# A streaming encoder layer on one core: which queue loads the first constants, how the first unit's chain is laid out, how the residual arrives, and who loads head 0

## The chip, the cores and the metric

The kernel runs as one program on one core of a Trainium2 chip. A core has five engines with a queue of instructions each, which is worked through in order: PE (TensorE, the matrix engine), DVE (VectorE), ACT (ScalarE), POOL (GpSimd) and SP (SyncE, which here only issues transfers). Any of SP, ACT and POOL can issue a transfer (DMA); the transfers of all queues are carried by the same 16 DMA engines. An instruction that waits holds up everything behind it on its own engine, and nothing else.

The metric is the device time of one execution in microseconds (us), lower is better. The kernel before has a median of 1366.96 us over three runs (1365.69 to 1368.74).

## The reference

One layer of a hybrid encoder over a prompt of 1024 frames and a sample of 32 frames, 1056 columns of width 1024 in all. Cut to its core:

```python
mod = jax.nn.silu(c) @ w_ada + b_ada
sh1, sc1, g1, sh2, sc2, g2 = jnp.split(mod[:, None, :], 6, axis=-1)
h = x * (1 + sc1) + sh1
mq, mk, mv, mo, mi, mf, fq, fk, fv, ff, gu, gv = jnp.split(h @ w_in, split_at, axis=-1)
hm, (C1, n1, m1) = _mlstm(heads(mq), heads(mk) * HEAD_DIM ** -0.5, heads(mv), li, lf, st0, blk)
hm = _head_norm(hm) * mlstm_norm_g * jax.nn.sigmoid(heads(mo))
hf = _fox_prompt(heads(fq), fk_h, fv_h, logf)      # softmax attention with a forget decay, 8 heads
hg = _spatial_gate(gu, vn, gmlp_ws, gmlp_bs)
mix = jnp.concatenate([hm, hf, hg], axis=-1) @ w_o
x = _layer_norm(ALPHA * x + (1 + g1) * mix, ln1_g, ln1_b)
h = x * (1 + sc2) + sh2
y = (jax.nn.silu(h @ w_gate) * (h @ w_up)) @ w_down
x = _layer_norm(ALPHA * x + (1 + g2) * y, ln2_g, ln2_b)
```

Everything is in float32. A product is made of three matmuls: each operand is split into a high part in the matrix engine's reduced format and the remainder (low), and high x high, high x low and low x high are added up.

## The kernel before

**Layout.** Activations lie transposed: 128 features on the partitions, frames on the free axis. A 1024 x 128 slice of a weight is loaded as one tile of 128 x 1024 (512 KB, `raw`), ACT copies it into the high part (`whi`, line 104) and DVE subtracts to get the low part (`wlo`, line 105). `gemm` (lines 116, 117, 118) then issues three matmuls for each of the eight blocks of the contraction.

**What sets the order.** The program is written once, from top to bottom, for tiles of named pools; a scheduler that goes by its own modelled times then lays each engine's instructions out in one fixed order and sets the semaphores. `issue_after(x)` keeps instructions behind x in that order. A pool's memory may lie where an earlier pool's lay that has been closed; its first writers then wait for the last users of the old tiles.

**The start.** `constants` loads two small tables on SP's queue, `colp` (biases and scales) and `cT` (the condition c), whose silu is needed by every ada unit. `fm_first` makes the first unit of the input projection, for eight blocks k of the contraction: `ada(k)` multiplies c with two halves of `w_ada` (512 KB each, 4 matmuls each, line 178), turns the result with two transposes (line 184), and adds the bias (lines 186, 192); `h1(k)` loads block k of x (540 KB) and makes h = x * (1 + scale) + shift on DVE (lines 216, 217) and its high and low parts on ACT and DVE (lines 221 to 224); then come 18 matmuls for block k. The unit's weights (two loads of 512 KB) are asked for behind block 0's h.

**Up to the first layer norm.** Further units of the projection follow, whose results go to tables in HBM (`dqh`, `dql`, `dmo`, `dmv` and others), then the first mixers (mLSTM, FoX, gMLP) for the first 512 columns. Their outputs come back from HBM with `wo_mix` (tiles `tm_al`, `tm_ah`); `wo_res` fetches the residual x into the 128 x 8 x 512 tile z (`wo_z`) with four loads of 512 KB; `wo_range` multiplies with `w_o` for 8 blocks m, first for columns 0 to 255, then 256 to 511, and `sublayer_end` adds the result to z on DVE (line 1066). `ln1` normalises on DVE and ACT (lines 1083 to 1092), while PE works on the last units of the projection; those are the fm units whose results are copied to the output o_kT by way of the tile `fm_qkr` in pool `sm` (on POOL's or ACT's queue). `ln1_res` then scales z once more on POOL (line 1101, 16 instructions), for the residual of the block after it.

**The second fox.** Pool `mx1` opens on the right side, where `p1` and `sm` lay. `mixers` runs the mixers of the other columns as many small pieces woven into the matmuls of SwiGLU (`up`). `fox(0)` loads head 0's queries, keys and decays with eight transfers and its values with a ninth (lines 747 to 755, SP's queue): qp and k1 first, which the first two score matmuls (line 779) need, then q2 and k2 for the next two (line 780). `mlstm` loads its pieces (`mv`, `mo`, `mb`), again on SP, and prepares the output gate from `mo` on ACT (lines 607 to 609). `ada` goes on in this region: one unit's result is copied by ACT (line 181) and turned on PE (line 184).

Of the kernel before, what the change touches and what calls it, by code (L numbers as in the profile page):

```python
# [63 lines left out]
def f(ap):  # L64
    return ap.bitcast(F32)


class Kernel:
# [14 lines left out]

    def load(self, out, in_):
        self.lastload = self.nc.sync.dma_start(out, in_)
        return self.lastload
# [34 lines left out]
    def constants(self):  # L121
# [48 lines left out]
    def ada(self, u, pool, tag, bufs, ppool, ptag):  # L170
        self.phase = "ada"
        nc = self.nc
        ps = self.t(ppool, [P, 512], F32, ptag)
        for half in range(2):
            raw = self.t(pool, [P, 1024 if tag == "late" else 1056], F32, tag, bufs)[:, :1024]
            self.load(raw, self.d["w_ada"][u, :, half * 1024:(half + 1) * 1024])
            for k in range(4):
                nc.tensor.matmul(ps[32 * k:32 * k + 32, :256], self.c32[:, 4 * half + k, :],
                                 raw[:, k * 256:(k + 1) * 256], start=half == 0, stop=half == 1)
        a = self.t(self.pada, [P, 256], F32, "adas", 2)  # L180
        nc.scalar.copy(a, ps[:, :256])
        pt = ps[:, 256:512]
        for half in range(2):
            nc.tensor.transpose(pt[:, half * P:(half + 1) * P], a[:, half * P:(half + 1) * P], self.ident)
# [23 lines left out]


    def h1(self, k):  # L210
        nc = self.nc
        x = self.t(self.p0, [P, T], F32, "x", XB)
        self.lastx = self.load(x, self.d["xT"][k])
        sh, sc = self.modcol("sh1", k), self.modcol("sc1", k)
# [28 lines left out]
    def fm_first(self, src):  # L243
# [4 lines left out]
                 ((self.pg, "g"), (self.pg, "g"), (self.pg, "g"), (self.pss, "s"), (self.pss, "s"), (self.po, "o"))]  # L248
        w = None
        self.ada(0, self.p0, "araw", AB, self.pt, "t")  # L250
        for k in range(KT):
# [128 lines left out]

    def decay(self, out, h, rows, tiles):
        j0, j1 = tiles
        self.load(f(out).rearrange("p (j q) -> p j q", q=P),
                  self.dfs.rearrange("(j h) r q -> h r j q", h=8)[h, rows, j0:j1])

# [351 lines left out]
    def fox(self, h, chunks):  # L737
# [6 lines left out]
        else:  # L744
            k1, k2, qp, q2, v = self.head_tiles(h, nq, nk)
            qs = slice(q0, q1)
            self.load(f(qp[0:64]), self.dqh[h, 0:64, qs])
            self.load(f(qp[64:128]), self.dql[h, 0:64, qs])
            self.load(f(k1[0:64]), self.dqh[h, 64:128, :nk])
            self.load(f(k1[64:128]), self.dqh[h, 64:128, :nk])  # L750
            self.load(f(q2[0:64]), self.dqh[h, 0:64, qs])
            self.decay(q2[64:68], h, slice(2, 6), (chunks[0][0], nb))
            self.load(f(k2[0:64]), self.dql[h, 64:128, :nk])
            self.decay(k2[64:68], h, slice(0, 4), (0, nb))
            self.load(f(v), self.dv[:, :nb, h * P:(h + 1) * P])
# [287 lines left out]
    def wo_range(self, st, a, b, order, kept, pool):  # L1043
# [293 lines left out]
    def run(self):  # L1337
# [120 lines left out]
        self.wo_mix(0, self.KORDER[0][6:])  # L1458
        self.wo_res(0, self.pz)
        self.pn = self.pool("pn")  # L1460
# [224 lines left out]
```

## Time and profile before

| | |
|---|---|
| median of three runs | 1366.96 us |
| the profiled execution | 1366.61 us, of which 1364.7 us are the span of the trace |
| PE busy | 1330.3 us (97%) |
| DVE, ACT, POOL busy | 995.4 (73%), 656.7 (48%), 226.6 us (17%) |
| granted clock of PE | 0.995 of full speed over the span |

Times in the trace are counted from the start of the span; the 1.9 us around it do not show. "Idle before" in a row of the timeline is the time in which the engine had nothing to do before this instruction, with the instruction or transfer that ended it. PE is idle for 34.4 us in all: 9.28 us in the first 20 us, 2.9 us in 300 to 380, 1.7 us in 380 to 400, 4.9 us in 445 to 462, and 12.15 us behind 1200 us; nowhere else is it more than 1 us in 40.

### The profile page before, as it was taken

What the parts mean: (1) busy time and instruction counts of PE and PEld (TensorE: products, weight loads), DVE (VectorE), ACT (ScalarE), POOL (GpSimd) and SP (SyncE); (2) the same over time, 40 slices, a digit from 0 to 9 for tenths busy, and PEclk for the clock granted to TensorE, in tenths of its full rate; (3) what the DMA queues carried; (4) which work ended last, traced back from release to release, by engine and by line L of the source; (5) the groups of instructions that cost most, each with busy time, mean ns of one, the idle gap of its engine ahead of it and who ended that gap; (6) DMA issues with size and microseconds to landing.
All of it is one profiled execution on the core that took longest, in us unless ns stands there. A gap on an engine that the chain in (4) does not pass through costs nothing.

```text
span 1364.7 us, 25185 instructions
## 1 busy us (share of the span) xinstructions
PE 1330.3 (97%) x9434; PEld 1215.8 (89%) x9434; DVE 995.4 (73%) x2129; ACT 656.7 (48%) x1306; POOL 226.6 (17%) x263
## 2 busy tenths in 40 slices
PE   7999999999999899999999999999999999999996
PEld 4898889998989777888887888999999999999995
DVE  5545553679769667786776765678988988879777
ACT  3314454545536554545545354336664554645355
POOL 0202000053134200000000000373710000000341
PEclk9999999999999899999999999999999999999998
DMA  9765565547454765454344334574596758454321
GB/s 359 273 231 152 161 206 154 163 138 212 134 201 135 207 189 171 119 154 134 109 122 120 104 110 130 156 181 124 164 254 170 205 149 223 146 170 127 99 79 66
DMA packets 119289, 221.70 MB, mean 162 GB/s; under 512 B 18676, under 2 KB 62352, under 8 KB 119168
## 3 DMA queue, kind: packets, MB, share of 16 engines
q1 hardware_dynamic: 111936, 207.55, 48.9%
q0 software_dynamic: 6032, 11.94, 5.1%
q8 instruction: 74, 1.21, 0.4%
q10 hardware_dynamic: 1200, 0.62, 0.2%
q14 instruction: 47, 0.39, 0.1%
HBM read 188.13 MB, written 51.85 MB: 176 GB/s over the span
## 4 chain that ended last, share of the span: by engine, by line
PE 84%; DVE 7%; DMA 5%; ACT 2%; issue 1%; SPq 1%; POOL 1%; DVEq 0%; ACTq 0%
PE up_g L117 5%; PE up_g L118 5%; PE up_g L116 5%; PE dn_g L116 4%; PE dn_g L118 4%; PE dn_g L117 4%; PE tm_g L281 3%; PE tm_g L282 3%; PE tm_g L283 3%; PE sup_u L118 3%; PE sup_u L116 3%; PE sup_u L117 3%; PE fox_t L815 2%; PE sup_g L117 2%; PE sup_g L118 2%; PE sup_g L116 2%
## 5 line engine op out<-in xcount | busy, mean ns | idle before, releaser
L117 PE MATMUL up_g<-tm_al,up_whi 128*128 128x512 f32 (+1 forms) x384 | 141.0, 367 | 0.5 <-DVE tm_al L1092 0.5
L116 PE MATMUL up_g<-tm_ah,up_whi 128*128 128x512 f32 (+1 forms) x384 | 141.2, 369 | 0.2
L118 PE MATMUL up_g<-tm_ah,up_wlo 128*128 128x512 f32 (+1 forms) x384 | 140.5, 366 | 0.0
L1211 ACT CAST sup_whi<-sup_raw 128x1024 fp32r<-128x1024 f32 x54 | 56.0, 1048 | 90.3 <-PE dn_u L117 46.7
L116 PEld LDWEIGHTS up_g<-tm_ah,up_whi 128*128 128x128 f32 x384 | 72.7, 190 | 12.5 <-ACT tm_ah L1091 0.6
L117 PEld LDWEIGHTS up_g<-tm_al,up_whi 128*128 128x128 f32 x384 | 73.1, 190 | 11.1 <-DVE tm_al L1092 0.7
L118 PEld LDWEIGHTS up_g<-tm_ah,up_wlo 128*128 128x128 f32 x384 | 73.2, 191 | 10.7
L788 ACT ACTIVATE fox_p<-fox_s,fox_fmx 128x384 f32<-128x384 f32 (+2 forms) x96 | 55.1, 578 | 44.8 <-DVE fox_fmx L786 37.4
L104 ACT CAST up_whi<-up_raw 128x1024 fp32r<-128x1024 f32 x50 | 52.4, 1048 | 49.7 <-PE up_g L117 19.0
L1212 DVE TENSOR_TENSOR sup_wlo<-sup_raw,sup_whi 128x1024 fp32r<-128x1024 f32 x54 | 68.2, 1267 | 10.5 <-ACT sup_whi L1211 10.5
L1066 DVE SCALAR_TENSOR_TENSOR wo_z<-dn_g,start_mod,wo_z 128x512 f32<-128x512 f32 (+4 forms) x120 | 60.3, 521 | 20.1 <-PE dn_g L118 19.7
L105 DVE TENSOR_TENSOR up_wlo<-up_raw,up_whi 128x1024 fp32r<-128x1024 f32 x50 | 65.7, 1314 | 11.6 <-ACT up_whi L104 11.0
L116 PE MATMUL dn_g<-up_acth,dn_whi 128*128 128x512 f32 (+2 forms) x200 | 74.1, 371 | 0.0
L118 PE MATMUL dn_g<-up_acth,dn_wlo 128*128 128x512 f32 (+2 forms) x200 | 73.4, 367 | 0.0
L117 PE MATMUL dn_g<-up_actl,dn_whi 128*128 128x512 f32 (+2 forms) x200 | 72.9, 365 | 0.0
L820 ACT CAST fox_pth<-fox_t 128x512 fp32r<-128x512 f32 (+1 forms) x80 | 41.0, 545 | 59.5 <-PE fox_t L815 59.3
L104 ACT CAST dn_whi<-dn_raw 128x1024 fp32r<-128x1024 f32 (+1 forms) x44 | 42.7, 971 | 52.2 <-PE up_g L117 10.7
L783 DVE TENSOR_REDUCE fox_fmx<-fox_s 128x1 f32<-128x384 f32 (+2 forms) x96 | 52.7, 553 | 13.0 <-PE fox_s L780 11.8
L821 DVE TENSOR_TENSOR fox_ptl<-fox_t,fox_pth 128x512 fp32r<-128x512 f32 (+1 forms) x80 | 49.5, 631 | 14.5 <-ACT fox_pth L820 14.4
L105 DVE TENSOR_TENSOR dn_wlo<-dn_raw,dn_whi 128x1024 fp32r<-128x1024 f32 (+1 forms) x44 | 49.5, 1125 | 13.7 <-ACT dn_whi L104 13.2
L281 PE MATMUL tm_g<-tm_whi,start_h1h 128*128 128x256 f32 (+1 forms) x192 | 55.3, 288 | 1.7 <-ACT tm_vhl L711 1.7
L282 PE MATMUL tm_g<-tm_wlo,start_h1h 128*128 128x256 f32 (+1 forms) x192 | 55.1, 287 | 0.0
(667 smaller groups left out, 4806.8 us busy)
## 6 DMA issues: line engine op xcount, KB each, us to landing
up_raw<-w_gu SPq DMA_DIRECT2D x50, 512.0 KB
dn_raw<-w_dn SPq DMA_DIRECT2D x28, 512.0 KB
ada_late<-w_ada SPq DMA_DIRECT2D x24, 512.0 KB
sup_raw<-w_gu SPq DMA_DIRECT2D x20, 512.0 KB
start_dp<-w_gu SPq DMA_DIRECT2D x19, 512.0 KB
start_dp<-w_gu POOLq DMA_DIRECT2D x19, 512.0 KB, 7.5
wo_raw<-w_o SPq DMA_DIRECT2D x18, 512.0 KB
sup_raw<-start_dp SPq DMA_DIRECT2D x18, 512.0 KB
```

The lines of the kernel that those rows point to most:

```text
L104: nc.scalar.copy(hi[:, :w], raw[:, :w])
L105: (eng or nc.vector).tensor_tensor(lo[:, :w], raw[:, :w], f(hi[:, :w]), ALU.subtract)
L116: nc.tensor.matmul(ps, hi, xh(k), start=start and k == 0, stop=False)
L117: nc.tensor.matmul(ps, hi, xl(k), start=False, stop=False)
L118: nc.tensor.matmul(ps, lo, xh(k), start=False, stop=stop and k == n - 1)
L281: nc.tensor.matmul(ps[:, :ncol], xh, hi, start=k == 0, stop=False)
L282: nc.tensor.matmul(ps[:, :ncol], xh, lo, start=False, stop=False)
L783: nc.vector.tensor_reduce(mxs[:, x:x + 1], s[:, :w], AX.X, ALU.max, negate=True)
L788: nc.scalar.activation(pr[:, lo:hi], banks[x][:, :hi - lo], AF.Exp, bias=mxs[:, 0:1], accum_out=sums[:, x:x + 1])
L1066: self.lastz = self.nc.vector.scalar_tensor_tensor(z[:, m, x:y], ps[:, x - a:y - a], g[i], z[:, m, x:y], ALU.mult, ALU.add)
L1211: nc.scalar.copy(h, x)
L1212: tt(l, x, f(h), ALU.subtract)
```

## The change

Four places are changed.

1. `constants`: cT and then colp are loaded by ACT's queue instead of SP's.
2. `fm_first`: ada(0) is followed at once by the load of x's block 0 and of the first half of the unit's weights (512 KB, four blocks of the contraction), which is split in four pieces of 256 columns, each with its own copy on ACT and subtraction on DVE. ada(1) stands behind ada(0)'s transposes on PE. The second half of the weights is fetched at k = 3, behind block 3 of x.
3. `wo_res` takes a range of columns and two blocks at a time, 256 KB a load. For columns 0 to 255 these loads stand between the loads of `w_o`; those of the second range behind the weights of m = 5 and m = 7.
4. Head 0's eight loads go by POOL's queue (only those of h = 0; the values' load stays on SP). `ln1_res(0)` is written behind the mixers and after these loads. The pools `sm` and `p1` swap places on the right side, so that the first tiles of `mx1`, head 0's, no longer lie over `sm`.

```diff
+    def load(self, out, in_, eng=None):
+        if eng:
+            self.lastside = eng.dma_start(out, in_)
+            return self.lastside
...
-        self.load(self.colp, d["colp"])
-        self.load(self.ct, d["cT"])
+        nc.scalar.dma_start(self.ct, d["cT"])
+        nc.scalar.dma_start(self.colp, d["colp"])
...
+            self.turned = nc.tensor.transpose(pt[:, half * P:(half + 1) * P], a[:, half * P:(half + 1) * P],
+                                              self.ident)
...
-        w = None
         self.ada(0, self.p0, "araw", AB, self.pt, "t")
+        self.x = self.first_x(0)
+        raw, hi, lo = (self.t(self.wp, [P, 1056], y, x, b) for x, y, b in
+                       (("raw", F32, RAW), ("whi", F32R, WB), ("wlo", F32R, WB)))
+        self.load(raw[:, :1024], src[:, :1024])
+        w = []
+
+        def split(k):
+            c = slice(256 * k, 256 * k + 256)
+            self.nc.scalar.copy(hi[:, c], raw[:, c])
+            self.nc.vector.tensor_tensor(lo[:, c], raw[:, c], f(hi[:, c]), ALU.subtract)
+            w.append((hi[:, c], lo[:, c]))
+
+        split(0)
+        with self.tc.issue_after(self.turned.ins):
+            self.ada(1, self.p0, "araw", AB, self.pt, "t")
         for k in range(KT):
-            if k < KT - 1:
+            if 1 <= k < KT - 1:
                 self.ada(k + 1, self.p0, "araw", AB, self.pt, "t")
             self.h1(k)
-            if w is None:
-                w = self.weights(src, KT, 256)
+            if k == 0:
+                for i in range(1, 4):
+                    split(i)
+            if k == 3:
+                with self.tc.issue_after(self.lastx.ins):
+                    w += self.weights(src[:, 1024:], 4, 256)
...
+            eng = self.nc.gpsimd if h == 0 else None
-            self.load(f(qp[0:64]), self.dqh[h, 0:64, qs])
+            self.load(f(qp[0:64]), self.dqh[h, 0:64, qs], eng)
...
-    def wo_res(self, c, pool):
-        z = self.z[c] = self.t(pool, [P, KT, GN[c]], F32, f"z{c}", 1)
-        for k in range(0, KT, 2):
-            self.load(z[:, k:k + 2], self.d["xT"][k:k + 2, :, GO[c]:GO[c] + GN[c]].rearrange("k p n -> p k n"))
+    def wo_res(self, a, b, k):
+        self.load(self.z[0][:, k:k + 2, a:b], self.d["xT"][k:k + 2, :, a:b].rearrange("k p n -> p k n"))
...
+            if a == 0 and m % 2 == 0:
+                self.wo_res(a, b, m)
             w = kept.get(m) or self.weights(self.d["w_o"][m], KT, P, None, pool if m < 3 else None)
+            if a == 0 and m in (5, 7):
+                with self.tc.issue_after(self.lastload.ins):
+                    for k in ((0, 4), (6, 2))[m // 7]:
+                        self.wo_res(*MM[0][1], k)
...
+        self.sm = self.pool("sm", 2, ctx=s1, side="right")
         self.p1 = self.pool("p1", ctx=s1, side="right")
-        self.sm = self.pool("sm", 2, ctx=s1, side="right")
...
-        self.ln1_res(0)
...
         self.mixers()
+        with tc.issue_after(self.lastside.ins):
+            self.ln1_res(0)
```

The scheduler makes other orders of it. Three places follow; the numbers in the names tell tiles apart and mean nothing else.

**The start, on DVE.** From the mods of unit 0 to the parts of block 0's h. Before:

```order
L186 TENSOR_REDUCE ada_adam_208<-ada_t_191 128x4
L192 TENSOR_SCALAR start_mod_156<-ada_adam_208,start_colp_108 128x2 x2
L216 TENSOR_SCALAR ada_h_235<-ada_x_233,start_mod_156 128x1024
L217 TENSOR_SCALAR ada_h_235<-ada_x_233,start_mod_156 128x32
L186 TENSOR_REDUCE ada_adam_229<-ada_t_212 128x4
L192 TENSOR_SCALAR start_mod_156<-ada_adam_229,start_colp_108 128x2 x2
L222 TENSOR_TENSOR start_al_170<-ada_h_235,start_ah_169 128x512
```

Now:

```order
L269 TENSOR_TENSOR fm_wlo_216<-fm_raw_214,fm_whi_215 128x256
L190 TENSOR_REDUCE ada_adam_208<-ada_t_191 128x4
L269 TENSOR_TENSOR fm_wlo_216<-fm_raw_214,fm_whi_215 128x256
L196 TENSOR_SCALAR start_mod_156<-ada_adam_208,start_colp_108 128x2 x2
L269 TENSOR_TENSOR fm_wlo_216<-fm_raw_214,fm_whi_215 128x256 x2
L225 TENSOR_SCALAR ada_h_241<-ada_x_212,start_mod_156 128x1024
L226 TENSOR_SCALAR ada_h_241<-ada_x_212,start_mod_156 128x32
L231 TENSOR_TENSOR start_al_170<-ada_h_241,start_ah_169 128x512
```

The four subtractions of the weights' first half now stand ahead of h and between the steps of unit 0's mods; unit 1's mods went behind.

**The w_o stage, on SP.** From the last mixer tile on (`dqh`, `dql` are stores of the projection). Before:

```order
L85 DMA tm_al_4640<-start_dmix_32_88 128x512
L85 DMA wo_z_895_4890<-xT 128x2x512 x4
L85 DMA wo_raw_5023<-w_o 128x1024
L85 DMA wo_raw_5060<-w_o 128x1024
L89 DMA start_dqh_57<-fm_qkh_4840 128x272
L85 DMA wo_raw_5097<-w_o 128x1024
```

Now:

```order
L88 DMA tm_al_4646<-start_dmix_32_88 128x512
L88 DMA wo_z_895_4896<-xT 128x2x256 x2
L88 DMA wo_raw_5027<-w_o 128x1024
L88 DMA wo_z_895_4896<-xT 128x2x256
L88 DMA wo_raw_5065<-w_o 128x1024
L88 DMA wo_z_895_4896<-xT 128x2x256
L92 DMA start_dqh_57<-fm_qkh_4846 128x272
L88 DMA wo_raw_5102<-w_o 128x1024
```

Two loads of 256 KB instead of four of 512 KB stand ahead of the first `wo_raw`.

**Head 0 of the second fox, on PE and ACT.** On PE from the last matmuls ahead of the first score (`fox_s`). Before:

```order
L116 MATMUL up_g_7925<-tm_ah_4639,up_whi_7838 128x256
L779 MATMUL fox_s_5854<-fox_k_1018_5837,fox_qp_5839 128x384
L779 MATMUL fox_s_5858<-fox_k_1018_5837,fox_qp_5839 128x256
L117 MATMUL up_g_7900<-tm_al_4640,up_whi_7832 128x256
L118 MATMUL up_g_7900<-tm_ah_4639,up_wlo_7833 128x256
```

Now:

```order
L121 MATMUL up_g_7935<-tm_ah_4645,up_wlo_7849 128x256
L181 MATMUL ada_g_7967<-ada_raw_7974,start_c_63_182 32x256 x4
L808 MATMUL fox_s_5848<-fox_k_1018_5831,fox_qp_5833 128x384
L808 MATMUL fox_s_5852<-fox_k_1018_5831,fox_qp_5833 128x256
L187 MATMUL ada_g_7967<-start_ident_121,ada_adas_7980 128x128 x2
L119 MATMUL up_g_8003<-tm_ah_4645,up_whi_7993 128x512
```

and on ACT the instructions around the copy `ada_adas`, which these two transposes read. Before:

```order
L1091 COPY tm_ah_4639<-lna_tmp_5587 128x256
L181 COPY ada_adas_7970<-ada_g_7957 128x256
L104 COPY up_whi_7989<-up_raw_7987 128x1024
```

Now:

```order
L1124 COPY tm_ah_4645<-lna_tmp_5597 128x256
L635 ACTIVATE mlstm_mo_6163<-mlstm_mo_6163 128x256
L636 ACTIVATE mlstm_mo_6163<-mlstm_mo_6163,start_ones_36_112 128x256
L107 COPY up_whi_7999<-up_raw_7997 128x1024
L1172 ACTIVATE up_sil_7902<-up_g_7910 128x256
L637 ACTIVATE mlstm_mo_6163<-mlstm_mo_6163 128x256
L646 ACTIVATE mlstm_mw_6202<-mlstm_mw_6202,start_col_178 128x128 x4
L1173 ACTIVATE up_sil_7902<-up_sil_7902,start_ones_36_112 128x256
L184 COPY ada_adas_7980<-ada_g_7967 128x256
```

All matmuls of the pair `up_g_7910`, `up_g_7935` now stand ahead of the first score, and the transposes of an ada unit right behind it; on ACT the gate of the mLSTM (`mlstm_mo`) and a weight's copy went ahead of `ada_adas`. PE's order is otherwise the same from the end of the first unit up to here.

More of the change, by code (lines that the diff above doesn't have):

```diff
@@ L82, in t @@
         return pool.tile(shape, dt, tag=tag, name=f"{self.phase}_{tag}_{self.n}", **kw)
-    def load(self, out, in_):
+    def load(self, out, in_, eng=None):
+        if eng:
+            self.lastside = eng.dma_start(out, in_)
+            return self.lastside
         self.lastload = self.nc.sync.dma_start(out, in_)
@@ L207, in parts, with first_x @@
         return ((lo, 512, 0), (512, hi, 1)) if lo < 512 else ((lo, hi, 1),)
+    def first_x(self, k):
+        x = self.t(self.p0, [P, T], F32, "x", XB)
+        self.lastx = self.load(x, self.d["xT"][k])
+        return x
     def h1(self, k):
         nc = self.nc
-        x = self.t(self.p0, [P, T], F32, "x", XB)
-        self.lastx = self.load(x, self.d["xT"][k])
+        x = self.x or self.first_x(k)
+        self.x = None
         sh, sc = self.modcol("sh1", k), self.modcol("sc1", k)
@@ L379, in evac_qk, with decay @@
         return evac
-    def decay(self, out, h, rows, tiles):
+    def decay(self, out, h, rows, tiles, eng=None):
         j0, j1 = tiles
         self.load(f(out).rearrange("p (j q) -> p j q", q=P),
-                  self.dfs.rearrange("(j h) r q -> h r j q", h=8)[h, rows, j0:j1])
+                  self.dfs.rearrange("(j h) r q -> h r j q", h=8)[h, rows, j0:j1], eng)
     def head_tiles(self, h, nq, nk):
@@ L746, in fox @@
             qs = slice(q0, q1)
-            self.load(f(qp[0:64]), self.dqh[h, 0:64, qs])
[L748 to L754, printed above, removed]
+            eng = self.nc.gpsimd if h == 0 else None
+            self.load(f(qp[0:64]), self.dqh[h, 0:64, qs], eng)
+            self.load(f(qp[64:128]), self.dql[h, 0:64, qs], eng)
+            self.load(f(k1[0:64]), self.dqh[h, 64:128, :nk], eng)
+            self.load(f(k1[64:128]), self.dqh[h, 64:128, :nk], eng)
+            self.load(f(q2[0:64]), self.dqh[h, 0:64, qs], eng)
+            self.decay(q2[64:68], h, slice(2, 6), (chunks[0][0], nb), eng)
+            self.load(f(k2[0:64]), self.dql[h, 64:128, :nk], eng)
+            self.decay(k2[64:68], h, slice(0, 4), (0, nb), eng)
             self.load(f(v), self.dv[:, :nb, h * P:(h + 1) * P])
```

4 lines of the change are left out of this document (2 added, 2 removed).

## The prediction

> **What bounds the kernel now.** I read the page first, then busy time by stretches, then what ended PE's pauses in the stretches where it pauses, and last the order of events there.
>
> ```profile
> PE 1330.3 (97%) x9434; PEld 1215.8 (89%) x9434; DVE 995.4 (73%) x2129; ACT 656.7 (48%) x1306; POOL 226.6 (17%) x263
> 0.00:20.00 20.00, 10.72 (x59) 5.35 (x60) 9.58 (x34) 6.37 (x11) 1.88 (x12) 1.00 0.88 325
> 380.00:400.00 20.00, 18.29 (x147) 17.58 (x147) 14.86 (x23) 7.83 (x12) 8.19 (x9) 1.00 0.68 235
> 445.00:456.00 11.00, 10.32 (x89) 8.98 (x88) 10.31 (x27) 9.65 (x24) 7.37 (x8) 1.00 0.45 138
> 456.00:462.00 6.00, 1.77 (x11) 1.59 (x11) 0.92 (x3) 0.43 (x2) 1.81 (x3) 0.78 0.79 186
> 1200.00:1364.70 164.70, 152.55 (x1194) 150.51 (x1192) 129.78 (x243) 76.91 (x122) 33.83 (x31) 0.98 0.33 102
> ```
>
> The columns are the stretch, its length, busy PE, PEld, DVE, ACT and POOL, PE's granted clock, the share of the DMA engines and GB/s. PE is the bound: 1364.7 - 1330.3 = 34.4 us of pauses are all that a change of order can win, and 12.15 of them lie in the tail, which this change does not touch. It can touch 9.28 us at the start, 1.3 in the w_o stage and 4.9 around 456; to these comes time at half clock.
>
> **The start.** First PE's waits up to 60 us, then the rows of PE, ACT, DVE and SP:
>
> ```profile
> PE ada_t L178 <- DMA ada_araw<-w_ada: 6.8, 2, 5.9
> PE fm_g L116 <- ACT fm_whi L104: 1.9, 1, 1.9
> ...
> 10.67 1.08 PE L178 MATMUL ada_t<-ada_araw,start_c 128*32 128x256 f32 x8
> 12.24 0.69 PE L184 MATMUL ada_t<-start_ident,ada_adas 128*128 128x128 f32 x2 [0.49 <-ACT ada_adas L181]
> 14.84 0.80 PE L116 MATMUL fm_g<-start_ah,fm_whi 128*128 128x512 f32 x1 [1.92 <-ACT fm_whi L104]
> 18.66 0.77 PE L178 MATMUL ada_t<-ada_araw,start_c 128*32 128x256 f32 x8
> ...
> 12.56 0.62 ACT L221 CAST start_ah<-ada_h 128x512 fp32r<-128x512 f32 x1 [0.38 <-DVE ada_h L216]
> 13.75 1.99 ACT L104 CAST fm_whi<-fm_raw 128x1024 fp32r<-128x1024 f32 x2
> ...
> 11.71 0.81 DVE L216 TENSOR_SCALAR ada_h<-ada_x,start_mod 128x1024 f32<-128x1024 f32 x1 [0.29 <-DMA ada_x<-xT]
> 14.86 2.35 DVE L105 TENSOR_TENSOR fm_wlo<-fm_raw,fm_whi 128x1024 fp32r<-128x1024 f32 x2
> ...
> 0.75 0.39 SPq L85 DMA_DIRECT2D start_colp<-colp  x1
> 1.66 1.85 SPq L85 DMA_DIRECT2D ada_araw<-w_ada  x4
> ...
> 4.00:14.00 10.00, 5.56 (x36) 1.42 (x36) 2.66 (x10) 2.18 (x6) 0.00 (x0) 1.00 1.01 379
> ```
>
> Without the two tables SP's first weight goes out at 0.75 instead of 1.66. The queue is full from 4 us on (share 1.01, 379 GB/s), so bytes decide the rest. x's block 0 was the fifth 0.5 MB and h waited for it at 11.7; now it is the third, 1.0 MB / 0.379 = 2.8 us earlier and 0.9 on top: about 8.1. The half of the weights, the fourth, comes 1.4 us later, 9.5. Then four copies (each a quarter of 1.99 / 2, so 0.25) and, behind the first, four subtractions (each a quarter of 2.35 / 2, 0.3) fill DVE to 11, and with unit 0's mods and the hand-overs between them, as the order has it, to about 12.0, which is my estimate; only then comes h. From h's start to the end of its part `ah` it takes 12.56 - 11.71 + 0.62 = 1.5: the first fm matmul is at 13.6, 1.24 earlier. PE's two transposes of unit 1, which ran in a pause at 12.24, now stand between fm matmuls: 0.69 less their overlap is 0.6 taken back. The same eight ada matmuls take 1.08 at 10.67 and 0.77 at 18.66: there the clock has just risen, 3.8 us behind the first fm matmul; ada(1) now runs until about 13.0 with little pause after it, so the ramp may end earlier by up to 2.7 us more, which would be worth half, 1.35. I take 0.4 of it, as where the ramp begins can't be read off one run. **Start: 1.24 - 0.6 + 0.4 = +1.0** (bounds -0.5, where block 7's h, which is last, stalls 1.1 and the ramp gives nothing, and +2.6).
>
> **The w_o stage.** PE's waits between 370 and 400, then SP and ACT:
>
> ```profile
> PE wo_g L116 <- ACT tm_ah L1003: 1.2, 1, 1.2
> PE wo_g L118 <- DVE wo_wlo L105: 1.1, 2, 0.8
> PE wo_g L116 <- ACT wo_whi L104: 0.6, 1, 0.6
> ...
> 371.34 3.41 SPq L85 DMA_DIRECT2D wo_z<-xT  x4
> ...
> 384.01 1.05 ACT L104 CAST wo_whi<-wo_raw 128x1024 fp32r<-128x1024 f32 x1 [5.68 <-DMA wo_raw<-w_o]
> ```
>
> The first wait is for the last mixer tile, ahead of the residual in the queue: it stays. The other two follow from a weight that lands at 384, behind 2 MB of residual. With 0.5 MB ahead of it instead, it comes 1.5 MB / 0.379 = 3.9 us earlier, and 0.6 + 0.8 = 1.4 go. The rest of the DVE row, 1.1 - 0.8, is a later weight's, whose load the change does not bring forward: it stays. **+1.4** (0.3, if DVE, busy with the results there, passes the wait on; 2.0 if the rest goes too). The second range's loads have some 10 us before their first use.
>
> **Head 0.** PE, SP and ACT around 456, and three stretches:
>
> ```profile
> 451.39 0.39 PE L117 MATMUL up_g<-tm_al,up_whi 128*128 128x256 f32 x1 [0.50 <-DVE tm_al L1092]
> 456.58 0.28 PE L118 MATMUL up_g<-tm_ah,up_wlo 128*128 128x256 f32 x1
> 456.70 0.28 PE L116 MATMUL up_g<-tm_ah,up_whi 128*128 128x256 f32 x1
> 461.21 0.87 PE L779 MATMUL fox_s<-fox_k,fox_qp 128*128 128x384 f32 x2 [4.23 <-DMA fox_k<-start_dqh]
> ...
> SPq L85 <- DMA o_kT<-fm_qkr: 3.4, 1, 3.4
> 454.06 0.47 SPq L85 DMA_DIRECT2D fox_qp<-start_dqh  x1
> 456.27 1.18 SPq L85 DMA_DIRECT2D fox_k<-start_dqh  x2
> ...
> 444.83 0.49 ACT L365 ACTIVATE fm_qkh<-fm_g,start_qsc 128x272 fp32r<-128x272 f32 x1 [1.10 <-PE fm_g L118]
> 465.32 1.05 ACT L104 CAST up_whi<-up_raw 128x1024 fp32r<-128x1024 f32 x1 [8.89 <-PE up_g L117]
> 470.03 0.41 ACT L607 ACTIVATE mlstm_mo<-mlstm_mo 128x256 f32<-128x256 f32 x1
> 471.04 1.27 ACT L618 ACTIVATE mlstm_mw<-mlstm_mw,start_col 128x128 f32<-128x128 f32 x4
> ...
> 448.63 4.90 POOL L1101 TENSOR_SCALAR wo_z<-wo_z,start_colp 128x256 f32<-128x256 f32 x3 [12.27 <-ACT lna_tmp L1087]
> L89 POOL DMA_DIRECT2D o_kT<-fm_qkr x4 | 2.2, 544 | 1.2 <-POOL fm_qkr L370 1.2
> ...
> 458.00:460.00 2.00, 0.00 (x0) 0.00 (x0) 0.00 (x0) 0.00 (x0) 0.00 (x0) 0.83 0.91 250
> 460.00:466.00 6.00, 4.79 (x21) 4.82 (x22) 0.54 (x3) 0.68 (x1) 0.00 (x0) 0.50 1.05 214
> 466.00:468.00 2.00, 2.00 (x10) 1.69 (x10) 1.72 (x4) 1.58 (x4) 0.00 (x0) 0.97 1.23 250
> ```
>
> SP waited 3.4 us for the landing of the last o_kT store, whose tile lay where head 0's now come; the keys landed at 461.1; PE stood 4.23 us, and the clock fell. By 0.83 over two us it was half for 0.7 of them, so from 459.3, 2.3 us into the pause; it came back at about 466.1, 4.9 us after the restart, and at half clock that costs 2.45. On POOL the eight loads wait only for the last fm matmul, 444.8 (where it releases ACT's `fm_qkh`), and at 0.54 each, as POOL's o_kT stores were issued between 365 and 412, they are out by 449.2; landing as slowly as the keys did (461.1 - 456.27 = 4.8), they are there by 454. POOL's line 1101 is out of their way. So the scores no longer wait.
>
> But the stall gets a new owner. PE's order now ends the `up_g` pair first (16 matmuls at 456.70 - 456.58 = 0.12, 1.87: until 458.85), does the two scores (0.3) and at 459.1 meets the transposes of `ada_adas`. On ACT that copy now stands behind the mLSTM's gate, and the gate's load stands on SP behind `mlstm_mv`, which takes over the wait for o_kT: mv at 454.06, a small load, `mo` at about 455.4. Landing 2.0 to 4.8 us after: 457.4 to 460.2. Then on ACT, in this order's rows: three steps of the gate, two of `up_sil` and the copy, 0.4 each, `up_whi` 1.05 and `mlstm_mw` 1.27, less what they overlap, together 4.3: ready at 461.7 to 464.5, which I take as 463.2. Even with `mo` there early, `up_whi` needs its buffer, free at 457.0: not before 461. The pause is 463.2 - 459.1 = 4.1 where 4.23 stood, and the clock falls again. **+0.1** (-1.3 to +1.6 from the two landings). POOL's scaling, gone from 448 to 454, frees DVE of what slowed it there, and the wait of 0.50 at 451.39: **+0.3** (0 to 0.5). Its 16 instructions now run behind 454 and nothing on PE wants them for tens of us.
>
> GpSimd issued those stores at 544 ns each beside a DVE that was busy. The Trainium skill ("SBUF — State Buffer", section "SBUF: two separate sides") speaks against this move: while DVE holds the shared port pair, GpSimd can't write its descriptors, and a load of 620 ns takes 3100. By that figure the last of the eight loads would, as an estimate, go out at 470 and land at 474. The trace's 544 ns does not agree with it.
>
> **The sum.** 1.0 + 1.4 + 0.1 + 0.3 = 2.8 from the profiled 1366.61 (0.35 below the median of the runs): **1363.8 us**. PE's order differs further on, until about the end of the fox heads; PE has hardly a pause there now, and I cost it at nothing.
>
> **The rivals.**
>
> *A. The pause really closes.* If `mo` lands by 457.3, the copy is done by 461.4 and the pause is 2.3 or less: the clock holds. Then 1.8 + 2.45 instead of 0.1: 1366.61 - 6.95 = 1359.7. For it: the early end of the range of landings just reaches it. Against: the DMA engines carry head 0's 1.2 MB just then. The Trainium skill ("TensorE: Matmul & The Clock Gate", Part 1) puts the idle window at about 3.4 us, free-running, so a pause up to that may keep the clock; here it fell after 2.3. By that rule 462.5 would do, and the time would be near 1361.
>
> *B. The new wait is longer than the old one (slower).* Head 0's loads (1.2 MB, 3.1 us at 379 GB/s) and the values' delay first the o_kT store that `mv` waits for and then `mo`. With both 2.5 to 3 later the copy ends at 469 and the pause is 10: 1363.8 + 5.8 = 1369.6. It turns slower than before at a copy later than 466, measurably so from 469.
>
> *C. The start gives nothing and the second pause stays.* The queue is saturated for 40 us; if the later blocks, not the first, set the unit's end, 1.0 goes and only 1.4 + 0.4 remain: 1364.8. For it: the same bytes still have to come. Against: behind the first 20 us PE pauses less than 1 us in 40.
>
> *D. The w_o wait is passed on too*, DVE being the next limit there: 1.1 less again, near 1366.
>
> *E. DVE holds up GpSimd's issues (slower).* POOL's own instructions took 4.90 / 3 = 1.6 each in 448 to 454, beside DVE's 10.31 busy of 11. At 1.6 a load the keys are still there by 456.1 and the last one by 462.6, where the second pair of scores, 19 matmuls behind the transposes, wants it at 468 at the earliest: nothing lost. At 2.3 each it lands just then, and every further 0.1 us a load costs 0.8: at 3.0 each, 1369.4. The Trainium skill's 3100 ns ("SBUF — State Buffer", same section) would make it 1370.
>
> **How the numbers follow.** Forecast 0.46, A 0.20, B 0.11, C 0.14, D 0.06, E 0.03. The forecast's own range, from the bounds of its terms taken together, is 1361.7 to 1366.0. Over all, A's time and the near part of B are taken in: 1359.5 to 1367.8. Runs of this kernel differ by about 0.2%, 2.7 us, so faster means below 1364.2 and slower above 1369.7. Faster: A and six tenths of the forecast and a little of C, 0.50; slower: half of B, E and a remainder for the changed order of the fox heads, 0.12; the same 0.38.
>
> **What would show it.** Right: the first fm matmul near 13.6 with DVE's four weight pieces ahead of h; no wait of PE for `wo_whi` and the first one near 380; head 0's loads done before 456; and PE's pause near 459 ended by ACT's `ada_adas`, with the clock at 0.5 behind it. Wrong: a pause that still ends with `fox_k`; a pause under 2.3 us; an `mlstm_mo` on ACT later than 462; new pauses of PE between 470 and 700.

## The result, and the profile after

| | before | after |
|---|---|---|
| median of the runs (nine each, side by side) | 1366.96 us (1364.72 to 1370.42) | 1371.78 us (1370.00 to 1375.49) |
| ratio, 95% interval | | 1.0041 (1.0030 to 1.0052) |
| profiled execution: span | 1364.7 us | 1370.0 us |

The change made the kernel slower by 0.4%, on the other side of the forecast of 1363.8 and outside the range of 1359.5 to 1367.8. An execution over 1.5% longer than the fastest of its kernel (one of only_head's took 3341.92 us) is left out of the medians below. The page's line of engine totals for the changed kernel:

```profile
PE 1334.8 (97%) x9434; PEld 1216.3 (89%) x9434; DVE 998.6 (73%) x2132; ACT 656.8 (48%) x1309; POOL 220.8 (16%) x271
```

PE runs the same 9434 matmuls, yet is busy for 4.5 us more. Its pauses grew by only 0.8 (1370.0 - 1334.8 = 35.2, against 34.4). Pauses won at one place and lost at another nearly cancel; what is left over is work that takes longer.

Where it arises comes out when each matmul is matched with itself in the trace of before. This is the median of start after minus start before, by place:

| place, us | difference | what changed since the row above |
|---|---|---|
| 60 to 160 | -0.1 | the start: nothing won |
| 345 | +2.1 | a stretch at half clock, 338.5 to 341.9, which before did not have |
| 400 to 445 | -0.7 to -0.9 | the w_o stage: 2.8 won |
| 860 | +5.5 | head 0 and the feed-forward work beside it: 6.3 lost |
| end | +5.2 | 0.3 won |

PE's waits of the changed kernel (engine, line, what it waited for; us in total, times, longest):

```profile
PE ada_t L181 <- DVE start_c L1414: 6.8, 1, 6.8
PE ada_g L187 <- ACT ada_adas L184: 6.4, 1, 6.4
PE ada_t L187 <- ACT ada_adas L184: 2.8, 5, 0.6
PE tm_g L309 <- ACT tm_vhl L739: 1.9, 1, 1.9
...
PE wo_g L119 <- ACT wo_qs L965: 0.8, 1, 0.8
```

The 4.2 us for `fox_k` are gone, and so are the waits for `wo_whi` and `wo_wlo`. In their place stand 6.4 us for `ada_adas`, the wait that the prediction named, and 0.8 for another operand of w_o.

**Head 0.** From the timeline of the changed kernel, PE, then ACT, SP and POOL around the pause (start, duration, instruction; in brackets the idle time before it and its releaser):

```profile
458.83 0.55 PE L808 MATMUL fox_s<-fox_k,fox_qp 128*128 128x384 f32 x2
465.83 0.69 PE L187 MATMUL ada_g<-start_ident,ada_adas 128*128 128x128 f32 x2 [6.44 <-ACT ada_adas L184]
...
461.48 0.42 ACT L635 ACTIVATE mlstm_mo<-mlstm_mo 128x256 f32<-128x256 f32 x1 [6.25 <-DMA foxs_k<-start_dsf]
465.42 0.35 ACT L184 COPY ada_adas<-ada_g 128x256 f32<-128x256 f32 x1
...
449.37 0.58 SPq L88 DMA_DIRECT2D fox_v<-start_dv  x1
449.99 0.80 SPq L88 DMA_DIRECT2D foxs_k<-cache_k  x1
450.84 0.60 SPq L88 DMA_DIRECT2D mlstm_mqk<-start_dmqk  x1
454.88 0.38 SPq L88 DMA_DIRECT2D mlstm_mv<-start_dmv  x1
456.07 0.42 SPq L88 DMA_DIRECT2D mlstm_mo<-start_dmo  x1
...
444.15 0.55 POOL L86 DMA_DIRECT2D fox_qp<-start_dqh  x1 [28.83 <-PE fm_g L121]
447.89 0.64 POOL L86 DMA_DIRECT2D fox_k<-start_dfs  x1
```

The scores wait for nothing. ACT's gate, which stands ahead of the copy, can start only at 461.48. From there to the end of the copy, at 465.77, it takes 4.3 us. The releaser in brackets is another load of SP's queue, issued 0.7 us ahead of `mo`. That is the last event the profile saw.

Stretches of 4 us, of before from 448 to 456 and then of after (stretch, length, busy PE, PEld, DVE, ACT, POOL, granted clock, DMA share, GB/s):

```profile
448.00:452.00 4.00, 3.45 (x27) 3.05 (x26) 3.70 (x9) 3.95 (x12) 3.37 (x1) 1.00 0.36 77
452.00:456.00 4.00, 3.86 (x39) 2.93 (x38) 3.61 (x9) 4.00 (x12) 4.00 (x8) 1.00 0.44 144
456.00:460.00 4.00, 0.97 (x8) 0.77 (x7) 0.92 (x3) 0.43 (x2) 1.81 (x3) 0.91 0.72 176
```

```profile
444.00:448.00 4.00, 4.00 (x36) 4.00 (x35) 4.00 (x13) 2.70 (x6) 3.85 (x8) 1.00 0.84 242
448.00:452.00 4.00, 3.32 (x20) 2.44 (x19) 3.64 (x8) 3.95 (x12) 0.52 (x1) 1.00 1.03 277
452.00:456.00 4.00, 3.54 (x31) 2.99 (x32) 3.18 (x9) 3.23 (x9) 0.87 (x3) 1.00 1.06 281
456.00:460.00 4.00, 3.39 (x30) 2.58 (x29) 0.00 (x0) 0.00 (x0) 4.00 (x8) 1.00 1.11 241
460.00:464.00 4.00, 0.00 (x0) 0.00 (x0) 1.40 (x2) 2.49 (x6) 4.00 (x8) 0.67 0.93 287
464.00:468.00 4.00, 2.08 (x5) 1.46 (x6) 2.83 (x8) 2.50 (x8) 2.62 (x3) 0.50 0.80 253
468.00:472.00 4.00, 4.00 (x11) 3.14 (x10) 0.98 (x1) 1.04 (x1) 0.00 (x0) 0.55 0.20 81
```

Two things are to be seen. The DMA engines were four tenths busy from 448 to 456 before; now they are full from 448 to 460 and move (277 + 281 + 241) x 4 = 3.2 MB there, against (77 + 144 + 176) x 4 = 1.6. Full means 241 to 281 GB/s here, where the start reached 400 with the engines as full (4 to 14 us, share 1.03): of the 1560 packets of 454 to 458, 1494 are under 2 KB, of the start's 1296 only 336. And PE's clock is at a half from about 461.5 to 471.7, 10.2 us, where it was 6.8 before.

### The profile page after: what moved, and what is told of

Same layout as the page of the kernel before. It is cut to its first block, busy times and chain, and to the rows that moved or that the text cites. A ratio compares the mean times of both kernels' runs of the same rounds, so it can differ in the third digit from the quotient of the medians.

```text
span 1370.0 us, 25212 instructions
## 1 busy us (share of the span) xinstructions
PE 1334.8 (97%) x9434; PEld 1216.3 (89%) x9434; DVE 998.6 (73%) x2132; ACT 656.8 (48%) x1309; POOL 220.8 (16%) x271
## 4 chain that ended last, share of the span: by engine, by line
PE 87%; DVE 4%; DMA 4%; ACT 2%; issue 1%; SPq 1%; ACTq 0%; DVEq 0%
PE up_g L119 6%; PE up_g L120 6%; PE up_g L121 6%; PE dn_g L119 4%; PE dn_g L121 4%; PE dn_g L120 4%; PE tm_g L309 3%; PE tm_g L310 3%; PE tm_g L311 3%; PE sup_u L121 3%; PE sup_u L119 3%; PE sup_u L120 3%; PE fox_t L844 2%; PE wo_g L120 2%; PE wo_g L119 2%; PE wo_g L121 2%
## 5 line engine op out<-in xcount | busy, mean ns | idle before, releaser
L812 DVE TENSOR_REDUCE fox_fmx<-fox_s 128x1 f32<-128x384 f32 (+2 forms) x96 | 52.7, 553 | 11.4 <-PE fox_s L809 10.2
```

Source lines behind the costliest of these rows:

```text
L812: nc.vector.tensor_reduce(mxs[:, x:x + 1], s[:, :w], AX.X, ALU.max, negate=True)
```

## The experiments

The theories at the outset: **theory 1**, the order of the queue: `mo` comes late because it is issued late, behind `mlstm_mv`, which waits for the o_kT store. **Theory 2**: most is lost later, from 500 on, where PE's order differs. A further one came out of the runs and is the one that stood, **theory 4**: moving head 0's loads to a second queue lets SP go on with 1 MB that nobody needs yet (head 0's values, the sample's keys and `mqk`); the engines are full, and what is needed first does not land first. In the table "P1" stands for parts 1 and 2 (the start), "P3" for the w_o stage, "P4" for head 0 with the swapped pools.

| run | what it is | median, us | ratio to before (95%) |
|---|---|---|---|
| only_start | before + P1 | 1366.40 | 1.0004 (.9991 to 1.0017) |
| only_wo | before + P3 | 1364.59 | .9989 (.9975 to 1.0003) |
| only_head | before + P4 | 1374.58 | 1.0052 (1.0036 to 1.0068) |
| head_sp | after, head 0's loads by SP | 1365.62 | .9993 (.9979 to 1.0007) |
| swap_only | before + swapped pools | 1365.49 | .9989 (.9976 to 1.0003) |
| wo_swap | before + P3 + swapped pools | 1364.44 | .9984 (.9974 to .9994) |
| sp_noconst | head_sp, constants by SP too | 1367.17 | .9997 (.9984 to 1.0010) |
| mv_pool | after, one load moved | 1373.66 | 1.0044 (1.0030 to 1.0058) |
| no_swap | after, pools not swapped | 1372.49 | 1.0047 (1.0033 to 1.0060) |
| mo_first | after, `mo` and `mb` first | 1363.75 | .9980 (.9967 to .9994) |
| wo_head_mo | mo_first without P1 | 1366.73 | .9998 (.9984 to 1.0011) |

### One part at a time

only_start, only_wo and only_head put parts of the diff shown above into the kernel before: the first two, the third and the fourth.

> The kernel before with the first and second part (constants on ScalarE's queue, first unit's chain). Theory 1: the first matmul of ada waits for c until about 6.7 instead of 5.85, because cT comes in beside two loads of 512 KB; the first fm matmul is near 13.1; PE is within 0.3 us of the kernel before from 60 us on; total within 1.5 us of before. Rival (the start gains and something later takes it away): 0.7 us or more ahead at 60.

> The kernel before with the third part alone (residual by range). Theory 1 (the new wait at head 0 is the loss, the w_o edit works): PE's waits for wo_whi and wo_wlo near 385 go, PE runs 1.3 to 2.9 us ahead of the kernel before from 400 on, the pause of 4.2 us for fox_k stays as it is; total 1 to 3 us below the kernel before. Rival (DVE passes the w_o wait on, so part 3 gives nothing and the gain seen there in the full change only made up for an earlier loss): less than 0.5 us ahead from 400 on, total within 1 us of before.

> The kernel before with the fourth part alone (head 0's loads on GpSimd, sm and p1 swapped, the scaling of z behind them). Theory 1: PE pauses about 6 us at 459 to 466 for ada_adas and runs at half clock for 2 or 3 windows of 3.4 us; 4 to 6 us behind by 500, total 4 to 7 us above before. Theory 2 (the changed order of the fox heads costs, not the pause): less than 3 us behind by 500 and 3 or more us lost between 500 and 860. Rival (the loss comes from the start or the w_o part moving the whole schedule): within 2 us of before.

The start is worth nothing that can be measured. The w_o part wins 1.8 us at its place (2.28 behind the profile of before at 360, 0.52 behind at 400). Only head 0 loses, and at least as much as the whole change: 0.5 ahead at 440, 4.2 us behind at 495, 4.6 at 507, 4.9 at 870. So **theory 2 falls**: little is lost from 500 on, 0.4 from 507 to 870. PE's wait in only_head and, below it, ACT's gate:

```profile
PE ada_g L187 <- ACT ada_adas L184: 6.0, 1, 6.0
...
461.97 0.42 ACT L611 ACTIVATE mlstm_mo<-mlstm_mo 128x256 f32<-128x256 f32 x1 [6.24 <-DMA mlstm_mo<-start_dmo]
```

Here the profile names the load itself: `mo`, issued at 456.36.

### Head 0's loads back on SP

```diff
-            eng = self.nc.gpsimd if h == 0 else None
+            eng = None
```

(and the residual behind SP's last load instead of GpSimd's).

> The full change, but head 0's eight loads stay on SP; the pools stay swapped and the scaling of z stays late. Theory 1 (the loss comes from what the scheduler makes of the loads on GpSimd: the ada copy behind the mLSTM gate): PE's order at head 0 is that of the kernel before, the loads no longer wait for the o_kT store, PE's pause for fox_k is under 2 us, no pause for ada_adas, no half clock near 460; total 1358 to 1363. Theory 3 (the swapped pools move the wait to mlstm_mv, and that wait decides whatever queue carries the loads): PE still loses 4 us or more between 450 and 500, total above 1366.

6 us come back, though not the 1358 to 1363 that I had expected. PE's order around head 0 is then that of before, and the wait for the keys is 0.9 instead of 4.2, with GpSimd out of it. The run is 6.4 us ahead of before at 469, but 0.9 from 518 on: PE waits 1.2 for `fox_ptl` and 1.1 for `fox_p`, and from 497.4 the clock is at half for 6.8 us. What had closed the old pause, then, is the rest of part 4, the swapped pools. Two more runs have them with head 0's loads on SP and the start of before:

```diff
-        self.p1 = self.pool("p1", ctx=s1, side="right")
         self.sm = self.pool("sm", 2, ctx=s1, side="right")
+        self.p1 = self.pool("p1", ctx=s1, side="right")
```

> The kernel before with sm and p1 swapped and nothing else; every engine's instructions stand in the same order as before. Theory 1: SP no longer waits for the o_kT store ahead of head 0's loads, so fox_qp goes out near 450.4 instead of 454.1 and the keys land by 457.5; PE's pause for fox_k is under 1.5 us instead of 4.2 and the clock does not fall at 459; 4 to 7 us ahead at 480, and at the end 4 to 7 us below before, or 1 to 2 where two pauses near 495 (for fox_p and fox_ptl, 2.3 us in the run with the loads on SP) bring the clock down there instead. Rival (the DMA engines are full there, so the keys land as late as before): pause 3.5 us or more, total within 1 us.

> The kernel before with the third part (residual by range) and the swapped pools; head 0's loads on SP, start as before, PE's order as before. Theory 1: the gains add up, 2 to 2.9 us at w_o and 4 to 7 at head 0 (or 1 to 2 if the clock falls near 495): total 1358 to 1364. Rival (what w_o wins is waited out again at head 0, since the o_kT store and the loads do not come earlier): no more than the better of the two parts alone.

With the order of every engine as before, the pause falls from 4.2 to 1.4 and the clock holds. PE's waits in swap_only from 440 to 510:

```profile
PE fox_s L784 <- DMA foxs_k<-start_dsf: 1.4, 1, 1.4
PE fox_o L828 <- DVE fox_ptl L826: 1.2, 1, 1.2
PE up_g L120 <- DVE tm_al L1097: 1.1, 1, 1.1
PE fox_t L820 <- DVE fox_p L801: 1.1, 1, 1.1
PE up_g L121 <- DVE up_wlo L108: 0.5, 1, 0.5
PE up_g L119 <- ACT up_whi L107: 0.3, 1, 0.3
```

So the old stall did come from the tile that lay where o_kT was read. But it is handed back: against before, swap_only is 1.4 us behind at 440, 3.6 ahead at 469 and level from 518 on. The waits for `fox_p`, `fox_ptl` and the up weights, between 468 and 506, were not there before: a PE that arrives earlier finds DVE and ACT not ready. wo_swap goes the same way: 6.4 ahead at 469, 2.4 from 518 on, 2.7 at the end. So the two gains did not add up: at 1364.44 it can't be told from only_wo (1364.59), as its rival had it.

### Where the loads of the start belong

sp_noconst is head_sp with the two constant tables loaded by SP, first in the queue as before.

> The full change with head 0's loads on SP and with the two constants on SP as before; beside the run that has the loads on SP alone it tells what the constants' queue costs. Theory 1 (on ScalarE's queue cT comes in beside 1 MB of other loads and c is ready 2.5 us later): ada starts near 5.9 instead of 6.7 and the first fm matmul comes at 12.3 to 13 with PE 0.3 to 1 us further ahead at 60 us. Rival (the first unit is bound by bytes, so the constants' queue does not matter): PE at 60 us within 0.3 us of the run with the loads on SP.

A miss: I had not expected the constants on SP to cost, and PE is 1.96 us behind before at 60 to 160, against 0.26 in head_sp. But wo_head_mo, whose start is that of before, is as late there in its profile (below), and the intervals of the two runs overlap. So where the constants belong stays open.

### Does `mo` come late because it is issued late?

mv_pool lets GpSimd issue the one load that waits for o_kT, so that `mo` need not stand behind it:

```diff
-        self.load(v[:L, :, 0:64], self.dmv[:L, j, :].rearrange("p (h e) -> p h e", h=4))
+        self.load(v[:L, :, 0:64], self.dmv[:L, j, :].rearrange("p (h e) -> p h e", h=4),
+                  nc.gpsimd if j == 4 else None)
```

> The full change, but the load of mlstm_mv of that one chunk is issued by GpSimd, so that mlstm_mo's load on SP does not stand behind the wait for the o_kT store; ACT's and PE's order around ada_adas stay as in the full change. Theory 1 (the chain o_kT, mv, mo, gate, ada_adas makes the pause): mo goes out near 451.5 instead of 456.1, the gate runs before 458, ada_adas is done at 461 to 462.5 and PE pauses 1.5 to 3.2 us instead of 6.4; total 3 to 5 us below the full change, 1366.5 to 1369. Rival (the pause comes from the weight's copy up_whi or from ACT being slowed, not from mo): pause 5 us or more, total within 1.5 us of the full change.

From its timeline, SP's issue, ACT's gate and PE behind it, and the stretch 456 to 460:

```profile
452.47 0.79 SPq L88 DMA_DIRECT2D mlstm_mo<-start_dmo  x1
...
461.94 0.42 ACT L636 ACTIVATE mlstm_mo<-mlstm_mo 128x256 f32<-128x256 f32 x1 [5.75 <-DMA mlstm_mo<-start_dmo]
...
466.43 0.69 PE L187 MATMUL ada_g<-start_ident,ada_adas 128*128 128x128 f32 x2 [6.10 <-ACT ada_adas L184]
...
456.00:460.00 4.00, 4.00 (x39) 3.04 (x33) 0.70 (x3) 0.19 (x1) 2.15 (x5) 1.00 1.15 254
```

**Theory 1 falls.** `mo` is issued 3.6 us earlier, and ACT still gets it at 461.9. What it waits for is not its turn to be issued; the next two runs ask whether it is the bytes ahead of it.

### Theory 4, from both sides

no_swap keeps the second queue and takes away the swapped pools, so that head 0's tiles wait for o_kT again; every engine's order is that of the change. mo_first keeps the whole change and puts the 128 KB of `mo`, and `mb`, ahead of SP's values, sample keys and `mqk` (`mo_mb` makes the same two loads):

```diff
+        self.early = self.mo_mb(4, P)
         for h in range(8):
...
-        mo = t([P, 256], "mo", 1)
-        self.load(mo[:L], self.dmo[:L, j, :])
-        mb = t([P, 4, P], "mb", 1)
...
+        mo, mb = self.mo_mb(j, L) if j != 4 else self.early
```

> The full change with sm and p1 not swapped; every engine's instructions stand in the same order as in the full change. Now GpSimd waits for the o_kT store ahead of head 0's loads, and SP does not wait ahead of mv. Theory 4: without head 0's loads beside it SP's queue is through by 456 to 458 and mo lands then, but head 0's keys land near 461, so PE waits for the scores (fox_qp or fox_k) for 1.5 to 3 us and hardly at all for ada_adas; the clock may fall; total 1366 to 1371. Theory 1 as first put (only the waits for the o_kT store matter): the same pause for the scores. Rival (the order alone costs it, wherever the waits lie): total as the full change, 1371 to 1374.

> The full change, but the loads of mlstm_mo and mlstm_mb of that chunk stand on SP ahead of head 0's values, the sample's keys and mqk; PE's order around the first scores is that of the full change. Theory 4 (SP's transfers land in their order, and mo lands late because of the loads ahead of it, 1 MB of values, keys and mqk mostly in packets of 512 bytes beside head 0's own, not because of when it is issued): mo lands by 456, the gate is done before up_whi, ada_adas is done at 458.5 to 460.5 and PE's pause there is under 1.5 us with no half clock at 460; total 3 to 7 us below the full change, 1365 to 1368.5. Rival (the copy ada_adas is late for another reason, such as the weight up_whi or ACT): pause 4 us or more and total within 1.5 us of the full change.

no_swap: ACT's gate, PE's score, and two stretches; then what the queues moved, q1 SP's and q0 GpSimd's (packets, MB, share of the engines), in the changed kernel from 454 to 458 and in no_swap from 454 to 458 and from 458 to 462.

```profile
460.80 0.42 ACT L635 ACTIVATE mlstm_mo<-mlstm_mo 128x256 f32<-128x256 f32 x1 [5.57 <-DMA mlstm_mo<-start_dmo]
...
465.79 0.87 PE L808 MATMUL fox_s<-fox_k,fox_qp 128*128 128x384 f32 x2 [6.89 <-DMA fox_k<-start_dqh]
...
456.00:460.00 4.00, 2.90 (x28) 2.28 (x27) 0.00 (x0) 0.00 (x0) 4.00 (x9) 1.00 1.16 284
460.00:464.00 4.00, 0.00 (x0) 0.00 (x0) 2.20 (x2) 3.17 (x8) 4.00 (x6) 0.98 1.07 243
...
q1 hardware_dynamic: 1553, 0.97, 114.5%
...
q1 hardware_dynamic: 1597, 0.99, 116.7%
...
q0 software_dynamic: 184, 0.59, 58.8%
```

GpSimd begins to issue head 0's loads at 454.7, within a microsecond of when SP did before (454.06), but the keys release the scores at 465.8 instead of 461.2. I had expected a wait of 1.5 to 3 us; it was 6.9. SP's megabyte, which used to stand behind the keys in one queue, now runs ahead of them: from 454 to 458 GpSimd's queue moves nothing. And `mo`, issued at 453.5, again lands near 461, where I had expected 456 to 458 without head 0's loads. So it is hardly those that hold it up; in the changed kernel too GpSimd's queue moves nothing from 454 on. What stands ahead of `mo` both times is SP's own megabyte. The total is that of the change, as the rival (the order alone costs it) has it; but with the same order on every engine PE's long wait is now for the keys and not for `ada_adas`, so the order alone does not set it.

mo_first: SP's issue, ACT's gate and its copy.

```profile
447.83 0.42 SPq L88 DMA_DIRECT2D fm_mo<-start_dmo  x1
...
454.24 0.42 ACT L639 ACTIVATE fm_mo<-fm_mo 128x256 f32<-128x256 f32 x1 [2.45 <-DMA fm_mo<-start_dmo]
460.17 0.37 ACT L184 COPY ada_adas<-ada_g 128x256 f32<-128x256 f32 x1 [0.21 <-PE ada_g L181]
```

The load took 6.4 us to land even so, but it began before the megabyte. The gate is done before anyone needs it, the copy is held only by PE's own matmul, and no pause of PE from 440 to 520 is longer than 0.6 us; the clock is at half once, for 3.4 us from 451.1. **8.0 us come back** (1371.78 to 1363.75), more than the 3 to 7 I had expected, and the kernel is 0.2% faster than before. Not all of it is the landing: the scheduler also ends the gate ahead of `up_whi` on ACT and lays out PE's `ada_g` matmuls in longer groups (below). It has the lowest median of all and beats both kernels; wo_swap, at 1364.44, can't be told from it.

### What stays open

wo_head_mo asks whether mo_first can do without the start.

> The same without the first two parts (start as before): residual by range, head 0 on GpSimd, mo and mb first. Theory 4 as above at head 0; since the start part was worth nothing, the total is within 1.5 us of the run with the start part, 1363 to 1368. Rival (the start part is worth something when nothing later takes it away): 1.5 us or more slower than that run.

It has no wait for `ada_adas` either, but is 3 us slower than mo_first. In its profile the untouched start came out 2.0 us late and the w_o work of the second half paused twice for 1.2, at 878 and 896; from 864 to 904 it loses 3.6 us, mo_first 0.1. As the start moved by up to 2 us between profiles of one code, I can't say which of the two it is; whether the start is worth half a microsecond is open with it.

## Why the prediction was wrong

**The step that failed: "Landing 2.0 to 4.8 us after: 457.4 to 460.2."** The steps beside it held. The scores wait no more; `mo` was issued at 456.07 (said: about 455.4); from gate to copy ACT took 4.3 us (said: 4.3); PE then waits for `ada_adas`, at half clock. But `mo` took until about 461.5, 5.4 us, and 9.5 and 7.3 us when it was issued earlier. I took landings from rows in which the queue was four to eight tenths full and carried them into a stretch that the change itself fills. Against the stated pause of 4.1 it is 6.4. That is **rival B**, at its place and with its sign, priced for a pause of 10. Its reason is only half right: the values' load delays `mo`, with the rest of SP's megabyte, but head 0's 1.2 MB hardly do, as no_swap shows. It had 0.11; the chance for it should have been most of it, because SP, rid of head 0's loads, sends its next megabyte ahead of `mo`.

All the signs of being right came: the first fm matmul at 13.08, no wait for `wo_whi`, the pause near 459 ended by `ada_adas` with the clock at half behind it. None of the signs of being wrong did (`mlstm_mo` at 461.48, said: not later than 462). They named places, and the places were right; the sizes were not.

The Trainium skill speaks against the second queue: "DMA: Bandwidth & Descriptors", section "Issuing engines are not separate DMA queues", has loads of all engines run and interleave on the same 16 DMA engines, a second issuer saving only issue time. no_swap agrees (keys 4.6 us later, behind SP's megabyte in the other queue).

**"+0.1 at head 0" was -6.3, and more than the pause.** The same 2592 matmuls from the last fm matmul to w_o's second half took 460.0 us before and 466.5 after. Of the 6.5 us, the pauses of PE account for 2.7 (6.4 + 0.6 + 0.4 against 4.2 + 0.5). The third stretch at half clock adds little, 0.5: more of it lies in the pause. And the step **"PE's order differs further on ... I cost it at nothing"** cost 1.9: from one start to the next, the 64 `ada_g` matmuls, which used to run in longer groups, are split up between others and take 5.9 us instead of 4.0, with the duration of each as before. One such group, before and then after, where other matmuls stand between the three parts:

```profile
478.41 1.07 PE L178 MATMUL ada_g<-ada_raw,start_c 128*32 128x256 f32 x16
...
480.56 0.63 PE L181 MATMUL ada_g<-ada_raw,start_c 128*32 128x256 f32 x6
...
482.03 0.63 PE L181 MATMUL ada_g<-ada_raw,start_c 128*32 128x256 f32 x4
...
482.95 0.63 PE L181 MATMUL ada_g<-ada_raw,start_c 128*32 128x256 f32 x6
```

These are sums of many rows, and some 1.4 us stay spread too thin to name. The +0.3 for POOL's scaling did not come either: the wait for `tm_al` is 0.4 where it was 0.5. In mo_first the same work takes 458.5, and these matmuls, in longer groups again, 4.1: both losses go back together.

**The start: +1.0 was +0.1; rival C had the size right.** What the term says does happen, even better: the first fm matmul is at 13.08 (said: 13.6), 1.76 earlier. But the table that ScalarE now loads lands later beside 1 MB of weights: the first rows of the changed kernel, then PE's first matmuls.

```profile
0.76 0.40 ACTq L130 DMA_DIRECT2D start_ct<-cT  x1
5.57 0.22 ACT L163 ACTIVATE start_ce<-start_ct 128x16 f32<-128x16 f32 x1 [2.61 <-DMA start_ct<-cT]
6.75 1.94 PE L181 MATMUL ada_t<-ada_araw,start_c 128*32 128x256 f32 x16 [6.75 <-DVE start_c L1414]
13.08 1.22 PE L119 MATMUL fm_g<-start_ah,fm_whi 128*128 128x512 f32 x2
```

4.8 us from issue to use, against 1.8 before (1.20 to 3.04). Up to 60 PE's pauses add up to 10.2 us, against 10.0 before. The 1.9 for `fm_whi` and 0.4 for `start_ah` are gone, but PE waits 0.9 longer at first, now for c, and 1.7 longer for ACT's copy `ada_adas` (four waits, 2.2 in all): the prediction priced the transposes that now stand between fm matmuls by their own length, not by the wait for the copy that they read. C's reason, that the bytes of the saturated queue set the end, does not show: from 14 to 60 ACT waits 0.3 us for a load, and PE and DVE not at all.

**The w_o stage: +1.4 was 2.8.** The mechanism is right and the sum too small. Stretches of before and after:

```profile
340.00:380.00 40.00, 38.82 (x318) 36.61 (x317) 28.71 (x77) 19.15 (x42) 8.60 (x14) 1.00 0.52 162
```

```profile
340.00:380.00 40.00, 40.00 (x322) 38.02 (x321) 28.91 (x78) 19.16 (x42) 8.58 (x14) 0.98 0.49 146
380.00:400.00 20.00, 19.17 (x160) 18.94 (x159) 16.09 (x25) 8.20 (x13) 7.60 (x10) 1.00 0.79 285
```

1.2 of PE's pauses are gone up to 380, the wait for `tm_ah` that I said would stay, and 0.9 up to 400, where 1.4 went and 0.8 came (`wo_qs`). The first is no merit of the change: PE arrived 2 us late, and a part of that lateness went into a wait that was there anyway. only_wo, which arrives on time, wins 1.8 and is the better size of this term. What makes up the remaining 0.7 I can't place.

**Not on my list: the clock at 338.** It fell for 3.4 us behind a pause of 1.90, a cost of 2.0; before, with a pause of 1.70 there, it held. The changes touch nothing near it. Of thirteen profiles two have it, and mv_pool, no_swap and mo_first, whose code up to there is that of the change, do not. So this belongs to the execution, not to the change.

**Rival E did not come about.** GpSimd issued each load in 0.52 to 0.64 us while DVE was busy for 4.00 of 4.00 us (444 to 448). The Trainium skill's 3100 ns ("SBUF — State Buffer", section "SBUF: two separate sides") do not show in this trace. **A** needed `mo` by 457.3 and **D** w_o passed on; neither was so.

## What to carry to other kernels

A second queue changes who issues a load, but the engines that carry it are the same: when they are full, the loads of both queues share them, and moving one queue's work aside lets the other's next megabyte start earlier, ahead of loads that are needed sooner. So before moving loads, list what the freed queue sends next, add up the bytes, and put what is needed first, first in its queue. And a wait that is closed on an engine of 97% is worth only what the engines behind it have ready: here most of the 5 us that the swapped pools won by 469 was handed back by 518.

## What the runs showed that I had not expected

The stretches at half clock, but for the one that each profile ends in, lasted 3.41, 6.83 or 10.24 us, one, two or three times 3.41; in the changed kernel the two falls (338.5 and 461.4) lie 36 times 3.413 apart. That agrees with the free-running window of 3413 ns of the Trainium skill ("TensorE: Matmul & The Clock Gate", Part 1), but its condition, an idle window of about 3.4 us, does not hold here: the clock fell behind stretches of 3.41 us with as little as 1.1 us of pause (mo_first, 447.7), and held behind others with 1.7 (swap_only, 336.6) and 2.0 (sp_noconst, 1354.0). So the length of the pause alone does not decide; what does, no run here settles.

The same small table took 1.8 us from issue to use ahead of the weights in SP's queue, and 4.1 (only_start) to 4.8 from ACT's queue with the weights issued at the same time. The queue and its company changed together, so no run tells which of the two it is.
